# Experts in 1024-column pieces, and the first expert's up projections as plain float32 matmuls in column tiles

## The chip, the core and the metric

The kernel runs on one core of a Trainium2 chip. A core has five engines, each with a queue of its own: TensorE (PE; its weight loads are shown as PEld), VectorE (DVE), ScalarE (ACT), GpSimd (POOL) and SyncE (SP), which here issues nearly all DMAs. The metric is the device time of one execution in microseconds (us), median of several runs; lower is better.

## The reference

Two decoder layers over 256 tokens of width 1024. Each has a mixer (gated recurrence, short convolution, merge) and a feed-forward part: a dense SwiGLU in layer 0, eight SwiGLU experts of inner width 2816 in layer 1, two for each token. The change touches only the experts:

```python
logits = jnp.einsum('td,de->te', t, router_w)
top_vals, top_idx = lax.top_k(logits, TOP_K)          # TOP_K = 2 of 8
gates = sum(one_hot(top_idx, 8) * softmax(top_vals))
for e in range(N_EXPERTS):
    a = t @ w1[e]                                     # 1024 -> 2816
    b = t @ w3[e]                                     # 1024 -> 2816
    out = out + gates[:, e:e + 1] * ((jax.nn.silu(a) * b) @ w2[e])
```

All of it is float32, 34.6 MB of weights for each expert.

## The kernel before

**Numbers.** TensorE has a one-pass type, float32r, that keeps fewer bits than float32. The kernel keeps float32 accuracy by splitting each operand into a high part `hi` and a low part `lo`, both float32r, and adding three products: hi·hi, hi·lo, lo·hi. Weights are split when they arrive. `wload` (L73) issues the DMA of one piece of 1 MB (128 partitions x 2048 elements, tile `wraw`) from SyncE, ScalarE copies it to `whi` (L86), VectorE makes `wlo = wraw - whi` (L88).

**Buffers.** `whi` has three buffers and `wlo` two. The `wraw` pieces go round a ring: four of a pool and a number of larger tiles that are idle just then; `more` puts such tiles in, `less` takes them out before the tile gets a use of its own.

**The experts** (`moe`, L739 to L978). The routing gives each expert up to 128 slots. `gather` multiplies one-hot matrices `P` (tile `sg`, made by `hot` at L794) with the token rows and so collects the rows of two experts at once, transposed and already in parts: `xh` and `xl`, 1024 rows in 8 tiles `kt` x 256 slots (tiles `bu`/`fc` and `kk`/`qq`; copies at L826, L828, L830). Then for every expert and every piece of the inner width (`FCH`: five of 512 columns and one of 256) the program issues

- `up_proj` of w1 (the gate) into `ab[:, 0]`: slots stationary, 512 weight columns moving, three matmuls for each `kt` (L881, L882, L883), two loads of four `kt` each;
- `turn` of the piece before: four transposes on PE (L890) and the split of the result into `ahe`, `ale` on ACT and DVE (L50, L51);
- `up_proj` of w3 (the up projection) into `ab[:, 1]`;
- `down` of the piece before: three matmuls for each 128 rows of w2 and each half of the width (L906 to L908) into `ye`, which gathers over all pieces of an expert;
- the activation: Silu on ACT (L976), the product on DVE (L977).

`ab` has two buffers in PSUM, so the next piece's `ab` is another buffer. After an expert's last piece `gated` scales `ye` (L933, L934), and after each second expert one-hot products put the rows back (L925).

**Order.** The program issues in this order; a scheduler moves instructions of one engine against each other where data allow it. Each engine then runs its list strictly in order. Before the first expert, `late` computes gates and the largest slot count, which SyncE reads (L987) between two weight loads.

The scores of the mixer are plain float32 matmuls, both operands `F32`. `scores` has the only ones that write a part of the partitions:

```python
rows = slice(2 * m * b, 2 * m * b + m)
for i in range(4):
    nc.tensor.matmul(ps[rows, i, b, :], kk[g][:, i, ...], qv[:, i, b, m:2 * m], ...)
```

At L359 with m = 32 these are 32 columns of the array, at rows 0 to 31 (b = 0) and 64 to 95 (b = 1); with m = 64 there are 64 columns at rows 0 to 63. At L338 the loop `for i in range(4)` over two token tiles makes 8 matmuls of 128 columns in a row.

Of the kernel before, what the change touches and what calls it, by code (L numbers as in the profile page):

```python
# [27 lines left out]
FCH = [(c, min(512, FF - c)) for c in range(0, FF, 512)]  # L28


@with_exitstack
def trunk_kernel(ctx: ExitStack, tc: tile.TileContext, x, w_in, lower_bounds, hgrn_norm_w, conv_w,
# [39 lines left out]
    def wload(src2d, k0, nk, c0, ncol):  # L72
        """rows k0*128.. (nk tiles) x columns c0..c0+ncol, split -> hi, lo [128, nk, ncol]"""  # L73
# [100 lines left out]
    # mean squares of the rows of the residual stream, by halves of the width  # L174
# [45 lines left out]
    # ---- the residual stream times a norm's weight, as columns in parts, by halves of the width. The  # L220
    # norm's factor of a token is applied to what is made of them: rstd by token, rbc as a row for all. ----
# [35 lines left out]
    def bounds():  # L257
        """lower bounds of the forget gates: cumulated softmax over the layers, less the first"""
# [33 lines left out]
    # within a block of 4, s <= t  # L292
# [6 lines left out]
    # s in the first, t in the second half of a block of 2m; t of the second halves only  # L299
# [85 lines left out]
    # o = S^T v, normalised per head, gated; token-major  # L385
# [89 lines left out]
    def route_slots(t):  # L475
        """1 + slot of the token within each expert, 0 where not chosen"""
# [6 lines left out]
    # ================= mixer =================  # L483
    def mixer(l):
# [13 lines left out]
        # forget gate, key, query: [key, head, t] in two groups of four heads  # L498
# [21 lines left out]
        # scores, transposed: [s, head, t]  # L520
# [12 lines left out]
        # output gate, token-major: silu(g) * norm weight  # L533
# [10 lines left out]
        # merge gates  # L544
# [12 lines left out]
        # short convolution: [channel, t]  # L557
# [30 lines left out]
        # projections and merge: [d, t]  # L588
# [21 lines left out]
        for g in range(2):  # L610
# [20 lines left out]
            # a token tile after the other, the routing of the first beside the second  # L631
# [25 lines left out]
    # ================= dense SwiGLU =================  # L657
    def dense(l):
# [10 lines left out]
        def down(c0, n, ah, al, w, dh, cs):  # L669
            """columns cs of the weights w, to the half dh of the width"""  # L670
# [11 lines left out]
        for ci, (c0, n) in enumerate(FCH):  # L682
# [15 lines left out]
            else:  # L698
                # the last two: one half of the width after the other
# [22 lines left out]
    # ================= final norm =================  # L722
# [12 lines left out]
    # ================= top-2 expert SwiGLU =================  # L735
    def moe(l):
# [8 lines left out]
        # the factors of a row: of its normalisation, and its gates; by token and by slot  # L745
# [11 lines left out]
        def make_gates():  # L757
            """softmax over the two kept logits"""
# [17 lines left out]
        def late():  # L776
            """what only the scatter needs: the gates, and the largest number of tokens of an expert"""
# [8 lines left out]
        def slots(base):  # L786
            """all experts on their slots base .. base+127"""
# [23 lines left out]
            def gather(e2, first=False):  # L811
# [3 lines left out]
                # one-hot products of the parts: exact  # L815
# [16 lines left out]
                if first:  # L832
                    # the first token tile ahead of the routing of the second
# [40 lines left out]
            def up_proj(src, c0, n, o, xh, xl, es):  # L874
                nh = (KT * n + 2047) // 2048
                per = KT // nh
                for half in range(nh):
                    wh, wl = wload(src, half * per, per, c0, n)
                    for k in range(per):
                        kt = half * per + k  # L880
                        nc.tensor.matmul(o, xh[:, kt, es], wh[:, k, :], start=kt == 0, stop=False)  # L881
                        nc.tensor.matmul(o, xh[:, kt, es], wl[:, k, :], start=False, stop=False)  # L882
                        nc.tensor.matmul(o, xl[:, kt, es], wh[:, k, :], start=False, stop=kt == KT - 1)  # L883

            def turn(e, c0, n, ci, sa, ys):
                """gated activations [slot, f] -> their parts [f, slot]"""
# [4 lines left out]
                ah = big.tile([128, nt, 128], F32R, tag=f"st{ci % 2}1", name="ahe")  # L891
                al = big.tile([128, nt, 128], F32R, tag=f"st{ci % 2}2", name="ale")
# [3 lines left out]
            def down(e, c0, n, ah, al, ys, PT, halves=(0, 1)):  # L896
                nt = n // 128
                for d0, dn in ([(h * 512, 512) for h in halves] if n == 512 else [(0, 1024)]):
                    wh, wl = wload(expert_w2[j, e], c0 // 128, nt, d0, dn)
                    for dh in range(dn // 512):  # L900
                        for k in range(nt):
                            o = ys[d0 // 512 + dh]
                            ds_ = slice(dh * 512, dh * 512 + 512)
                            first = c0 == 0 and k == 0
                            end = c0 + n == FF and k == nt - 1
                            nc.tensor.matmul(o, ah[:, k, :], wh[:, k, ds_], start=first, stop=False)  # L906
                            nc.tensor.matmul(o, ah[:, k, :], wl[:, k, ds_], start=False, stop=False)  # L907
                            nc.tensor.matmul(o, al[:, k, :], wh[:, k, ds_], start=False, stop=end)  # L908
# [27 lines left out]
            pend = None  # L936
# [7 lines left out]
            d_gather, p_gather = last["gather"], last["prod"]  # L944
            for e in range(NE):
# [4 lines left out]
                for ci, (c0, n) in enumerate(FCH):  # L950
# [3 lines left out]
                    ab = psum.tile([128, 2, 512], F32, tag="mm", name="ab")  # L954
                    up_proj(expert_w1[j, e], c0, n, ab[:, 0, 0:n], xh, xl, es)
# [6 lines left out]
                    if base == 0 and e == 0 and ci == 4:  # L962
                        less("tokA")
                    if e == 0 and ci == 3:
                        less("v")
                        PT = hot_t()
                    if pend is not None:
                        pend = turn(*pend)
                    up_proj(expert_w3[j, e], c0, n, ab[:, 1, 0:n], xh, xl, es)
                    if e % 2 == 1 and e + 1 < NE and ci == 2:  # L970
                        less("fc", "qq")
                        nxt = gather(e // 2 + 1)
                    if pend is not None and not final:
# [54 lines left out]
```

## Time and profile before

| | us |
|---|---|
| median of 3 runs (lowest, highest) | 1619.73 (1618.6, 1619.83) |
| span of the profiled execution, first to last instruction | 1618.9 |
| PE busy | 1594.9 |
| PEld busy | 1427.5 |
| DVE busy | 1243.7 |
| ACT busy | 938.4 |
| POOL busy | 33.9 |

For the profiled execution only its span is given, no time of its own; it lies within the three runs' range and 0.8 us under their median. The experts are worked on from about 826 us to 1605 us. Matmuls are pipelined: the profile models their ends, so that a row of 0.39 us may be followed by the next start 0.23 us later. What a matmul costs in a dense stream is read from starts.

### The profile page before, as it was taken

The numbers are of one execution on the slowest core, as the hardware profiler recorded it, in microseconds if no ns is written. First come the engines' busy times: TensorE is split into PE (matmuls) and PEld (weight loads), VectorE is DVE, ScalarE is ACT, GpSimd is POOL, SyncE is SP. The second block draws the span as 40 slices with busy tenths as digits, with TensorE's granted clock in tenths as the row PEclk, the third lists the DMA queues.
The fourth block names the chain that finished last, engine by engine and source line by source line (L and its number), as shares of the span: only waits on it lengthen the run. The fifth ranks groups of instructions, "written<-read, shape, count | busy, mean of one in ns | idle before, by whom it ended". The sixth has DMA issues, their size and how long they took to land.

```text
span 1618.9 us, 23572 instructions
## 1 busy us (share of the span) xinstructions
PE 1594.9 (99%) x9858; PEld 1427.5 (88%) x9858; DVE 1243.7 (77%) x1182; ACT 938.4 (58%) x836; POOL 33.9 (2%) x51
## 2 busy tenths in 40 slices
PE   7999999999999999999999999999999999999997
PEld 7989999999999989999988888888888888888886
DVE  6964785655446965677678898888888888888886
ACT  6434343544335444334467777677776777767775
POOL 2000020000000000010000000000000000000000
PEclk9999999999999999999999999999999999999998
DMA  7544445555654554458568999999999999999992
GB/s 276 183 158 164 149 132 187 180 182 181 201 189 162 177 182 156 157 195 286 171 221 311 352 324 331 337 366 373 339 356 331 364 374 346 365 334 365 373 376 97
DMA packets 215939, 417.06 MB, mean 258 GB/s; under 512 B 6528, under 2 KB 25056, under 8 KB 215824
## 3 DMA queue, kind: packets, MB, share of 16 engines
q1 hardware_dynamic: 215408, 414.25, 73.1%
q8 instruction: 79, 1.29, 0.3%
q0 software_dynamic: 384, 1.21, 0.2%
q14 instruction: 36, 0.29, 0.0%
q10 hardware_dynamic: 32, 0.01, 0.0%
HBM read 414.40 MB, written 1.05 MB: 257 GB/s over the span
## 4 chain that ended last, share of the span: by engine, by line
PE 96%; DVE 2%; ACT 1%; DMA 1%; issue 0%; POOL 0%; SPq 0%; POOLq 0%; DVEq 0%
PE psb L128 11%; PE psb L130 11%; PE psb L132 11%; PE ab L882 10%; PE ab L883 10%; PE ab L881 9%; PE ye L908 5%; PE ye L906 5%; PE ye L907 5%; PE psa L149 2%; PE psa L151 2%; PE psa L150 2%; PE psl L365 1%; PE y L677 1%; PE y L678 1%; PE y L679 1%
## 5 line engine op out<-in xcount | busy, mean ns | idle before, releaser
L86 ACT ACTIVATE whi<-wraw 128x2048 fp32r<-128x2048 f32 (+1 forms) x456 | 760.5, 1679 | 507.8 <-PE psb L130 257.6
L88 DVE TENSOR_TENSOR wlo<-wraw,whi 128x2048 fp32r<-128x2048 f32 (+1 forms) x456 | 900.1, 1993 | 199.7 <-ACT whi L86 93.1
L128 PE MATMUL psb<-hlA,whi 128*128 128x256 f32 x1376 | 393.2, 286 | 2.7 <-ACT hlA L217 2.7
L130 PE MATMUL psb<-hlB,whi 128*128 128x256 f32 x1376 | 390.5, 284 | 0.5 <-DVE hlB L218 0.5
L132 PE MATMUL psb<-hlA,wlo 128*128 128x256 f32 x1376 | 390.3, 284 | 0.0
L128 PEld LDWEIGHTS psb<-hlA,whi 128*128 128x128 f32 x1376 | 264.4, 192 | 3.9 <-ACT hlA L217 3.1
L130 PEld LDWEIGHTS psb<-hlB,whi 128*128 128x128 f32 x1376 | 264.6, 192 | 1.1 <-DVE hlB L218 0.7
L132 PEld LDWEIGHTS psb<-hlA,wlo 128*128 128x128 f32 x1376 | 264.5, 192 | 0.2
L882 PE MATMUL ab<-wlo,bu 128*128 128x512 f32 (+1 forms) x384 | 144.2, 375 | 1.2 <-DVE wlo L88 1.2
L882 PE MATMUL ab<-wlo,fc 128*128 128x512 f32 (+1 forms) x384 | 144.5, 376 | 0.8 <-DVE wlo L88 0.8
L881 PE MATMUL ab<-whi,bu 128*128 128x512 f32 (+1 forms) x384 | 144.2, 376 | 0.0
L881 PE MATMUL ab<-whi,fc 128*128 128x512 f32 (+1 forms) x384 | 143.8, 374 | 0.0
L883 PE MATMUL ab<-whi,kk 128*128 128x512 f32 (+1 forms) x384 | 143.0, 372 | 0.0
L883 PE MATMUL ab<-whi,qq 128*128 128x512 f32 (+1 forms) x384 | 142.9, 372 | 0.0
L907 PE MATMUL ye<-wlo,ahe 128*128 128x512 f32 x352 | 137.7, 391 | 0.7 <-DVE wlo L88 0.7
L908 PE MATMUL ye<-whi,ale 128*128 128x512 f32 x352 | 136.9, 390 | 0.2
L906 PE MATMUL ye<-whi,ahe 128*128 128x512 f32 x352 | 136.6, 390 | 0.0
L882 PEld LDWEIGHTS ab<-wlo,bu 128*128 128x128 f32 x384 | 72.4, 189 | 14.4 <-DVE wlo L88 2.8
L882 PEld LDWEIGHTS ab<-wlo,fc 128*128 128x128 f32 x384 | 72.3, 188 | 14.4 <-DVE wlo L88 2.7
L881 PEld LDWEIGHTS ab<-whi,fc 128*128 128x128 f32 x384 | 72.3, 188 | 12.6
L881 PEld LDWEIGHTS ab<-whi,bu 128*128 128x128 f32 x384 | 72.3, 188 | 12.3
L883 PEld LDWEIGHTS ab<-whi,kk 128*128 128x128 f32 x384 | 72.4, 188 | 12.1
(243 smaller groups left out, 1867.1 us busy)
## 6 DMA issues: line engine op xcount, KB each, us to landing
wraw<-in_expert_w_dram SPq DMA_DIRECT2D x264, 1024.0 KB, 6.8
wraw<-in_w_in_dram SPq DMA_DIRECT2D x72, 1024.0 KB, 5.0
wraw<-in_dense_w_dram SPq DMA_DIRECT2D x33, 1024.0 KB, 5.0
wraw<-in_w_proj_conv_dram SPq DMA_DIRECT2D x8, 1024.0 KB, 5.0
wraw<-in_w_proj_hgrn_dram SPq DMA_DIRECT2D x8, 1024.0 KB, 5.0
wraw<-in_w_out_dram SPq DMA_DIRECT2D x8, 1024.0 KB, 5.0
xt<-in_x_dram SPq DMA_DIRECT2D x2, 512.0 KB, 4.7
out_dram<-bu SPq DMA_DIRECT2D x4, 256.0 KB, 2.9
```

The costliest lines, as they stand in the source:

```text
L86: nc.scalar.activation(hf[:, ks], rf[:, ks], AF.Copy)
L88: nc.vector.tensor_tensor(lf[:, ks], rf[:, ks], hf[:, ks].bitcast(F32), op=ALU.subtract)
L128: nc.tensor.matmul(o, wh[:, k, cs], hh[:, kt, :], start=first, stop=False, skip_group_check=True)
L130: nc.tensor.matmul(o, wh[:, k, cs], hl[:, kt, :], start=False, stop=False, skip_group_check=True)
L132: nc.tensor.matmul(o, wl[:, k, cs], hh[:, kt, :], start=False, stop=last, skip_group_check=True)
L149: nc.tensor.matmul(o, hh[:, kt, ts], wh[:, k, :], start=kt == 0, stop=False)
L881: nc.tensor.matmul(o, xh[:, kt, es], wh[:, k, :], start=kt == 0, stop=False)
L882: nc.tensor.matmul(o, xh[:, kt, es], wl[:, k, :], start=False, stop=False)
L883: nc.tensor.matmul(o, xl[:, kt, es], wh[:, k, :], start=False, stop=kt == KT - 1)
L906: nc.tensor.matmul(o, ah[:, k, :], wh[:, k, ds_], start=first, stop=False)
L907: nc.tensor.matmul(o, ah[:, k, :], wl[:, k, ds_], start=False, stop=False)
L908: nc.tensor.matmul(o, al[:, k, :], wh[:, k, ds_], start=False, stop=end)
```

## The change

The experts' pieces become 1024 columns wide (`WIDE`: 1024, 1024, 768). A load is two `kt` of up to 1024 columns, with rows of 4 KB instead of 2 KB in memory; the number of float32r matmuls of an expert stays the same. The gate and the up product of a piece are now two PSUM tiles `pa` and `pb` of the tag that had two buffers for `ab`, so one piece's pair fills both. A piece is activated, turned and fed to `down` in two halves (`p`), one directly behind the other.

The first expert's two up projections are done without splits: `xf = xh + xl` (one DVE addition, 128x1024, into tile `fc`), the raw weights `wraw` as the moving operand, both plain float32, one matmul instead of three for each `kt` and 512 columns. But each is cut by slots: for the gate into two matmuls of 64 slots, for the up projection into four of 32, each on its own columns of the array and its own partitions of the output. Experts 1 to 7 keep the splits. Comment lines that the change also takes out, and shifted line numbers, are left out here.

```diff
+WIDE = [(c, min(1024, FF - c)) for c in range(0, FF, 1024)]
...
+    def wraw(src2d, k0, nk, c0, ncol):
+        r = from_ring("raw", raws, [128, nk, ncol], F32)
+        nc.sync.dma_start(r, src2d[k0 * 128:(k0 + nk) * 128, c0:c0 + ncol].rearrange("(k p) c -> p k c", p=128))
+        return r
...
             def up_proj(src, c0, n, o, xh, xl, es):
-                nh = (KT * n + 2047) // 2048
-                per = KT // nh
-                for half in range(nh):
-                    wh, wl = wload(src, half * per, per, c0, n)
...
+                for part in range(KT // 2):
+                    wh, wl = wload(src, part * 2, 2, c0, n)
+                    for k in range(2):
+                        kt = part * 2 + k
+                        for p in range(0, n, 512):
+                            ps_ = slice(p, min(p + 512, n))
+                            op = o[:, p // 512, 0:ps_.stop - p]
+                            nc.tensor.matmul(op, xh[:, kt, es], wh[:, k, ps_], start=kt == 0, stop=False)
+                            nc.tensor.matmul(op, xh[:, kt, es], wl[:, k, ps_], start=False, stop=False)
+                            nc.tensor.matmul(op, xl[:, kt, es], wh[:, k, ps_], start=False, stop=kt == KT - 1)
+
+            def up_full(src, c0, n, o, xf, lane):
+                for part in range(KT // 2):
+                    w = wraw(src, part * 2, 2, c0, n)
+                    for k in range(2):
+                        kt = part * 2 + k
+                        for p in range(0, n, 512):
+                            ps_ = slice(p, min(p + 512, n))
+                            for c in range(0, 128, lane):
+                                nc.tensor.matmul(o[c:c + lane, p // 512, 0:ps_.stop - p], xf[:, kt, c:c + lane],
+                                                 w[:, k, ps_], start=kt == 0, stop=kt == KT - 1)
...
+            def down(e, c0, n, ah, al, ys, PT):
+                for k0 in range(0, n // 128, 2):
+                    wh, wl = wload(expert_w2[j, e], c0 // 128 + k0, 2, 0, 1024)
...
+            if base == 0:
+                less("fc")
+                xf = big8("fc", [128, KT, 128])
+                nc.vector.tensor_tensor(xf, nxt[0][:, :, 0:128].bitcast(F32), nxt[1][:, :, 0:128].bitcast(F32), op=ALU.add)
...
-                for ci, (c0, n) in enumerate(FCH):
+                for ci, (c0, n) in enumerate(WIDE):
...
+                    pa = psum.tile([128, 2, 512], F32, tag="mm", name="ab")
+                    if e == 0 and base == 0:
+                        up_full(expert_w1[j, e], c0, n, pa, xf, 64)
+                    else:
+                        up_proj(expert_w1[j, e], c0, n, pa, xh, xl, es)
...
+                    pend = [turn(*x) for x in pend]
+                    pb = psum.tile([128, 2, 512], F32, tag="mm", name="ab")
+                    if e == 0 and base == 0:
+                        up_full(expert_w3[j, e], c0, n, pb, xf, 32)
+                    else:
+                        up_proj(expert_w3[j, e], c0, n, pb, xh, xl, es)
...
+                    def acts():
+                        return [activate(e, c0, n, p, pa, pb) + (ys,) for p in range((n + 511) // 512)]
```

How the order of instructions moves is seen at three places. The first is PE where the first expert begins; `pr` are the slot factors, `pp` the slot counts, `ppt` transposes of the one-hot matrices, `bu`, `kk` the tiles of `xh`, `xl`. Before:

```order
L819 MATMUL pg<-sg_7747,hlB 128x256 x6
L869 MATMUL pr<-rg,sg_7747 128x1 x4
L881 MATMUL ab<-whi,bu 128x512
L882 MATMUL ab<-wlo,bu 128x512
L883 MATMUL ab<-whi,kk 128x512
```

and of the change, from the same place:

```order
L826 MATMUL pg<-sg_7747,hlB 128x256 x6
L876 MATMUL pr<-rg,sg_7747 128x1 x4
L789 MATMUL pp<-sel,ones 128x8 x2
L811 MATMUL ppt<-ident,sg_7747 128x128 x4
L902 MATMUL ab<-wraw,fc 64x512 x32
L902 MATMUL ab<-wraw,fc 32x512 x64
L902 MATMUL ab<-wraw,fc 64x512 x32
```

The slot counts and the first four transposes now stand ahead of the first expert's products. A piece of 1024 columns is 32 matmuls for the gate (8 `kt`, two halves, two tiles) and 64 for the up projection; the last piece (768) is 16 of 512 and 16 of 256 columns for the gate, 32 and 32 for the up projection.

The second place is DVE at the same time. Before, the splits of the first loads (`wlo`) stand between the gather's copies and behind them:

```order
L88 TENSOR_TENSOR wlo<-wraw,whi 128x512 x2
L830 CAST kk<-pg 128x512 x2
L88 TENSOR_TENSOR wlo<-wraw,whi 128x512
L830 CAST kk<-pg 128x512
L872 COPY sc<-pr 128x2
L88 TENSOR_TENSOR wlo<-wraw,whi 128x512
L794 TENSOR_SCALAR sg_7747<-iota,posm 128x128 x12
```

Of the change:

```order
L837 CAST kk<-pg 128x512 x3
L879 COPY sc<-pr 128x2
L975 TENSOR_TENSOR fc<-bu,kk 128x1024
L801 TENSOR_SCALAR sg_7747<-iota,posm 128x128 x12
```

The splits are gone there, and the addition that makes `xf` (tile `fc`) stands behind the last copy and the slot factors, ahead of the other experts' one-hot matrices.

The third place is DVE within expert 2, where `sae` are activations and `ale` the low parts of turned ones. Before:

```order
L977 SCALAR_TENSOR_TENSOR sae<-ab,sc,sae 128x512
L88 TENSOR_TENSOR wlo<-wraw,whi 128x2048 x5
L51 TENSOR_TENSOR ale<-pta,ahe 128x512
L88 TENSOR_TENSOR wlo<-wraw,whi 128x2048
L977 SCALAR_TENSOR_TENSOR sae<-ab,sc,sae 128x512
```

Of the change:

```order
L910 SCALAR_TENSOR_TENSOR sae<-ab,sc,sae 128x512 x2
L89 TENSOR_TENSOR wlo<-wraw,whi 128x2048 x4
L52 TENSOR_TENSOR ale<-pta,ahe 128x512 x2
L89 TENSOR_TENSOR wlo<-wraw,whi 128x2048 x3
```

Work between the splits now comes in pairs, half as often.

## Rows read from the trace of the kernel before

**Rows 1.** The profile's page: busy time by engine, clock digits, chain that ended last.

```profile
PE 1594.9 (99%) x9858; PEld 1427.5 (88%) x9858; DVE 1243.7 (77%) x1182; ACT 938.4 (58%) x836; POOL 33.9 (2%) x51
...
PEclk9999999999999999999999999999999999999998
...
PE 96%; DVE 2%; ACT 1%; DMA 1%; issue 0%; POOL 0%; SPq 0%; POOLq 0%; DVEq 0%
```

**Rows 2.** Windows: length, busy us (instructions) by engine, PE clock, DMA share, GB/s.

```profile
1050.00:1100.00 50.00, 50.00 (x228) 41.42 (x227) 44.41 (x25) 37.75 (x24) 0.00 (x0) 1.00 1.04 369
1100.00:1150.00 50.00, 49.61 (x248) 41.60 (x247) 45.08 (x27) 37.18 (x27) 0.00 (x0) 1.00 0.99 356
```

**Rows 3.** Timeline of PE, 999.7 to 1003 us: start us, us, instruction.

```profile
999.73 0.39 PE L882 MATMUL ab<-wlo,bu 128*128 128x512 f32 x1
999.96 0.39 PE L883 MATMUL ab<-whi,kk 128*128 128x512 f32 x1
...
1002.91 0.39 PE L906 MATMUL ye<-whi,ahe 128*128 128x512 f32 x1
```

**Rows 4.** Timeline of PE at 1135 and 1330 us; in brackets its idle time before.

```profile
1135.22 0.50 PE L882 MATMUL ab<-wlo,fc 128*128 128x512 f32 x1 [0.39 <-DVE wlo L88]
...
1330.43 0.50 PE L882 MATMUL ab<-wlo,bu 128*128 128x512 f32 x1 [0.39 <-DVE wlo L88]
```

**Rows 5.** Waits, 826 to 1619 us: in total us, times, longest us.

```profile
PEld ab L882 <- DVE wlo L88: 5.5, 14, 1.2
...
PE ab L882 <- DVE wlo L88: 2.0, 4, 0.8
PEld ye L907 <- DVE wlo L88: 2.0, 4, 0.8
```

**Rows 6.** Timeline of PE at 21.7 us: split products of 256 columns, plain float32.

```profile
21.67 0.28 PE L128 MATMUL psb<-hlA,whi 128*128 128x256 f32 x1
21.79 0.28 PE L130 MATMUL psb<-hlB,whi 128*128 128x256 f32 x1
...
22.04 0.59 PE L242 MATMUL prb<-dg,ones 128*128 128x256 f32 x2
22.47 0.23 PE L195 MATMUL pcp<-ident,prow 80*128 80x80 f32 x1
```

**Rows 7.** Timeline of PE: 128 and 64 moving columns, then the next start.

```profile
88.70 1.95 PE L338 MATMUL psd<-qq,kk 128*128 128x128 f32 x16
90.40 0.48 PE L149 MATMUL psa<-whi,hlA 128*128 128x512 f32 x1
...
95.94 1.89 PE L365 MATMUL psl<-qq,kk 128*128 128x64 f32 x16
97.64 0.48 PE L149 MATMUL psa<-whi,hlA 128*128 128x512 f32 x1
```

**Rows 8.** Timeline of PE: the matmuls in 32 and in 64 columns.

```profile
118.08 0.69 PE L359 MATMUL psl<-qq,kk 128*32 128x32 f32 x16
...
125.76 1.15 PE L359 MATMUL psl<-qq,kk 128*64 128x64 f32 x16
126.83 0.39 PE L128 MATMUL psb<-hlA,whi 128*128 128x256 f32 x1
```

**Rows 9.** Timeline of DVE and PE where the first expert begins, and at 839 us.

```profile
826.01 0.69 DVE L830 CAST kk<-pg 128x512 fp32r<-128x512 f32 x1
826.80 0.16 DVE L872 COPY sc<-pr 128x2 f32<-128x2 f32 x1
...
826.62 0.48 PE L881 MATMUL ab<-whi,bu 128*128 128x512 f32 x1
...
838.05 0.39 PE L881 MATMUL ab<-whi,bu 128*128 128x512 f32 x1
839.23 0.50 PE L882 MATMUL ab<-wlo,bu 128*128 128x512 f32 x1 [0.80 <-DVE wlo L88]
```

**Rows 10.** Groups on DVE by shape: count, busy us, mean ns, idle before.

```profile
L977 DVE SCALAR_TENSOR_TENSOR sae<-ab,sc,sae 128x512 f32<-128x512 f32 x40 | 29.7, 743 | 0.0
...
L316 DVE TENSOR_TENSOR kk<-kk,fc 128x1024 f32<-128x1024 f32 x4 | 4.9, 1215 | 0.0
```

**Rows 11.** Timeline of ACT and DVE in an undisturbed stretch, 1089 to 1097 us.

```profile
1089.20 1.92 ACT L86 ACTIVATE whi<-wraw 128x2048 fp32r<-128x2048 f32 x1 [0.80 <-PE ye L908]
1091.16 2.29 DVE L88 TENSOR_TENSOR wlo<-wraw,whi 128x2048 fp32r<-128x2048 f32 x1 [0.38 <-ACT whi L86]
1093.87 2.29 DVE L88 TENSOR_TENSOR wlo<-wraw,whi 128x2048 fp32r<-128x2048 f32 x1 [0.43 <-ACT whi L86]
```

**Rows 12.** Windows around the routing; columns as in the second group.

```profile
815.00:818.70 3.70, 2.98 (x22) 2.49 (x22) 2.05 (x8) 2.01 (x5) 0.00 (x0) 1.00 0.74 218
818.70:825.50 6.80, 6.02 (x30) 5.93 (x29) 4.88 (x16) 3.44 (x8) 0.70 (x1) 0.50 0.52 194
```

More of the change, by code (lines that the diff above doesn't have):

```diff
@@ L874, in up_proj @@
             def up_proj(src, c0, n, o, xh, xl, es):
-                nh = (KT * n + 2047) // 2048
-                per = KT // nh
-                for half in range(nh):
-                    wh, wl = wload(src, half * per, per, c0, n)
[L879 to L883, printed above, removed]
@@ L887, in turn, with activate @@
+            def activate(e, c0, n, p, pa, pb):
+                m = min(512, n - p * 512)
+                sa = big.tile([128, m], F32, tag=f"st{p}0", name="sae")
+                nc.scalar.activation(sa, pa[:, p, 0:m], AF.Silu, scale=sc[:, e, 0:1])
+                nc.vector.scalar_tensor_tensor(sa, pb[:, p, 0:m], sc[:, e, 0:1], sa, op0=ALU.mult, op1=ALU.mult)
+                return e, c0 + p * 512, m, p, sa
+            def turn(e, c0, n, p, sa, ys):
                 nt = n // 128
@@ L890, in turn @@
                     nc.tensor.transpose(ps[:, k, :], sa[:, k * 128:k * 128 + 128], ident)
-                ah = big.tile([128, nt, 128], F32R, tag=f"st{ci % 2}1", name="ahe")
-                al = big.tile([128, nt, 128], F32R, tag=f"st{ci % 2}2", name="ale")
+                ah = big.tile([128, nt, 128], F32R, tag=f"st{p}1", name="ahe")
+                al = big.tile([128, nt, 128], F32R, tag=f"st{p}2", name="ale")
                 split(ps, ah, al)
                 return e, c0, n, ah, al, ys
[L896 to L902, printed above, removed]
-                            ds_ = slice(dh * 512, dh * 512 + 512)
[L904 to L908, printed above, removed]
+            def down(e, c0, n, ah, al, ys, PT):
+                for k0 in range(0, n // 128, 2):
+                    wh, wl = wload(expert_w2[j, e], c0 // 128 + k0, 2, 0, 1024)
+                    for k in range(2):
+                        for dh in range(2):
+                            o = ys[dh]
+                            ds_ = slice(dh * 512, dh * 512 + 512)
+                            first = c0 == 0 and k0 + k == 0
+                            end = c0 + n == FF and k0 + k == n // 128 - 1
+                            nc.tensor.matmul(o, ah[:, k0 + k, :], wh[:, k, ds_], start=first, stop=False)
+                            nc.tensor.matmul(o, ah[:, k0 + k, :], wl[:, k, ds_], start=False, stop=False)
+                            nc.tensor.matmul(o, al[:, k0 + k, :], wh[:, k, ds_], start=False, stop=end)
                 if c0 + n == FF:
@@ L934, in gated @@
                 nc.vector.scalar_tensor_tensor(y[1], src, g, y[0].bitcast(F32), op0=ALU.mult, op1=ALU.subtract)
-            pend = None
+            pend = []
             PT = None
@@ L953, in slots @@
                         ring["fine"] = 5
-                    ab = psum.tile([128, 2, 512], F32, tag="mm", name="ab")
-                    up_proj(expert_w1[j, e], c0, n, ab[:, 0, 0:n], xh, xl, es)
+                    pa = psum.tile([128, 2, 512], F32, tag="mm", name="ab")
[3 more added lines that the diff above has]
+                        up_proj(expert_w1[j, e], c0, n, pa, xh, xl, es)
                     if e == 0 and ci == 0:
@@ L961, in slots @@
                                 late()
-                    if base == 0 and e == 0 and ci == 4:
+                    if base == 0 and e == 0 and ci == 2:
                         less("tokA")
-                    if e == 0 and ci == 3:
+                    if e == 0 and ci == 1:
                         less("v")
                         PT = hot_t()
-                    if pend is not None:
-                        pend = turn(*pend)
-                    up_proj(expert_w3[j, e], c0, n, ab[:, 1, 0:n], xh, xl, es)
@@ L970, in slots @@
-                    if e % 2 == 1 and e + 1 < NE and ci == 2:
-                        less("fc", "qq")
-                        nxt = gather(e // 2 + 1)
-                    if pend is not None and not final:
-                        down(*pend, PT)
-                    sa = big.tile([128, n], F32, tag=f"st{ci % 2}0", name="sae")
-                    nc.scalar.activation(sa, ab[:, 0, 0:n], AF.Silu, scale=sc[:, e, 0:1])
-                    nc.vector.scalar_tensor_tensor(sa, ab[:, 1, 0:n], sc[:, e, 0:1], sa, op0=ALU.mult, op1=ALU.mult)
@@ L978, in slots @@
-                    if final:
-                        down(*pend, PT, [0])
-                        end = turn(e, c0, n, ci, sa, ys)
-                        down(*pend, PT, [1])
-                        down(*end, PT)
-                    pend = (e, c0, n, ci, sa, ys)
+                    pend = [turn(*x) for x in pend]
[4 more added lines that the diff above has]
+                        up_proj(expert_w3[j, e], c0, n, pb, xh, xl, es)
@@ new lines, in slots @@
+                    if e % 2 == 1 and e + 1 < NE and ci == 1:
+                        less("fc", "qq") if base == 0 and e > 1 else less("qq")
+                        nxt = gather(e // 2 + 1)
+                    def acts():
+                        return [activate(e, c0, n, p, pa, pb) + (ys,) for p in range((n + 511) // 512)]
+                    if not final:
+                        for x in pend:
+                            down(*x, PT)
+                        pend = acts()
+                        continue
@@ L985, in moe @@
+                    here = acts()
+                    for i, x in enumerate(pend):
+                        down(*x, PT)
+                        here[i] = turn(*here[i])
+                    for x in here:
+                        down(*x, PT)
         slots(0)
```

1 line of the change is left out of this document (removed).

## The prediction

> **What bounds the kernel now.** First the page: PE is busy 99% of the span, at a full clock but for short stretches, and 96% of the chain that ended last is PE's [rows 1]. Busy time proves little for PE, whose ends are modelled, so I read the stage that the change touches. In windows of 50 us PE is busy 49.6 to 50.0, DVE about 45, ACT about 38; the DMA share is about 1.0 [rows 2], so DMA, too, could be the bound. What decides is the spacing of PE's starts: from 999.73 to 1002.91 us lie 14 intervals, so a split product of 512 columns costs 3.18 / 14 = 0.227 us, one like the other [rows 3]. A PE that waited for data would be irregular. A larger test: the same place in the work comes again after 1330.43 − 1135.22 = 195.2 us, two experts [rows 4]. Two experts hold 2 x (5 x 8 x 2 x 3) = 480 products of 512 columns in the up projections and 264 in `down`, 744 x 0.227 = 168.9 us, and 96 of 256 columns at 0.12 (21.79 − 21.67 [rows 6]), 11.5 us. Transposes, gather and scatter come on top. That is 180.4 of 195.2 us before these are counted. What PE waits for `wlo` over all eight experts is small: 5.5 + 2.0 + 2.0 us in the larger groups, partly the same time seen by weight load and matmul [rows 5]. So the experts run at PE's own pace, and whatever lightens DVE, ACT or DMA can give back some 10 us at most.
>
> **What the change removes.** In the first expert's two up projections: 240 products of 512 columns and 48 of 256, 240 x 0.227 + 48 x 0.12 = 60.3 us of PE. Also their splits on ACT and DVE, which the rows above show to be off the path.
>
> **What it adds on PE.** A plain float32 matmul is two records in the trace: the program has 8 at L338, the trace 16 [rows 7]. Two records of 256 columns take 22.47 − 22.04 = 0.43 us [rows 6]; 16 of 128 columns take 1.70 [rows 7], 0.106 each, the same price per column. So a record of 512 columns is 0.43 us, one of 256 0.215. The gate's tiles of 64 slots make 80 matmuls of 512 and 16 of 256 columns: 160 x 0.43 + 32 x 0.215 = 75.7 us of streaming. The up projection's tiles of 32 make twice as many: 151.4. A narrow tile does not stream faster: with 64 array columns, 16 records of 64 moving columns take 1.07 us [rows 8], 0.067 each, no less than 64 / 256 x 0.215 = 0.054.
>
> So all depends on whether streams in different column tiles overlap. The kernel before never shows it: its only change of tile, in the middle of the 16 records at 118.08 [rows 8], lies among streams so short that a weight load is as long. (A load of 128 columns takes 0.106: 64 moving columns at L365 go no faster than 128 at L338 [rows 7]. By share, an estimate, 32 columns take 0.027 and their stream, also by share, 32 / 256 x 0.215 = 0.027.) The ends:
>
> - every tile's stream beside the others: the gate 75.7 / 2, the up projection 151.4 / 4, 75.7 us together, 15.4 more than the 60.3 removed;
> - all one after the other: 227.1 us, 166.8 more.
>
> I take a value between. In every row PE starts matmuls in the program's order, and a tile's two records stand next to each other. The second cannot stream before the first has left the tile; only then can the next tile's first record start, beside it. So two streams run at any time, however many tiles there are: 227.1 / 2 = 113.5 us, **53.2 more**. Of the rows, those on weight loads are nearest: PEld is busy 88% of the span beside a PE busy 99% [rows 1], so the array takes in new weights while it streams. If the load at each change of tile shows, 96 x 0.053 + 192 x 0.027 = 10 us come on top; I leave them to the range.
>
> The Trainium skill (TensorE: Matmul & The Clock Gate, Part 3: Packing small matmuls) has a rule that speaks against the change: weight loads overlap running matmuls only when the row group differs. Column tiles share all rows. By it all 192 records of the gate and 384 of the up projection would show their loads, 192 x 0.053 + 384 x 0.027 = 20.5 us, and the sum would be 74 instead of 53. The rows on loads show overlap within one full-width tile, which the rule does not have, so I stay with 53.
>
> **The start.** The first product before starts at 826.62, with its first `kt` in place. Now it needs all of `xf`: the last gather copy ends at 826.70, the slot factors take 0.16 [rows 9], the addition as a 128x1024 row 1.22 [rows 10], so about 828.1: **1.5 more**, though `pp` and four transposes fill part of it. Against it, the wait at 839.23 (0.95 longer than the spacing of 0.227 [rows 9]) goes with the splits: **−1.0**.
>
> **Experts 1 to 7.** As many products, the same streams: nothing on PE. Longer DMA rows have PE's pace as their cover; if that cover went, DMA at its present rate would still deliver. The pairs on DVE: in a quiet stretch DVE idles 0.43 us of each 2.72 (1093.87 − 1091.16) and waits for ACT, which waits for a free `whi` [rows 11]. With three such buffers a split done 0.2 + 1.92 + 2.29 = 4.4 us after a buffer came free is needed only 5.4 us after it, 1.0 to spare. Two activations of 0.743 in a row [rows 10] are 1.49: more than 0.43 + 1.0 by 0.06. I count 0.1 us for each of three pieces of seven experts: **2**. Bounds: −8, if nearly all waits for `wlo` went; +10, if each pair also held up ACT's next split by its 0.5. One pair of `pa` and `pb` fills both PSUM buffers, but Silu reads `pa` while PE works on the up projection and `down`, some 20 us: nothing.
>
> **Sum.** 53.2 + 1.5 − 1.0 + 2 = 55.7 on the profiled span of 1618.9, 1674.6; the median stands 0.8 over that span: **1675 us**.
>
> **Rivals.**
>
> *Column tiles don't overlap.* The change then does not do what its tiles are for. For it: the 16 records of [rows 8] keep one pace over their change of tile, 16 in 0.69 with the last one's tail. Against: that pace is what loads alone would give. 166.8 in place of 53.2: 1789 us.
>
> *All tiles stream together.* 15.4 in place of 53.2: 1638 us. For it: no row forbids it. Against: a tile's two records stand side by side in PE's list. The skill's page on TensorE (Part 3 again) stands for this one: tiles start about 4 ns apart, measured for three column tiles of 32 as a gain of 2.38. No run here shows it.
>
> *The clock falls.* From 818.70 to 825.50 the granted clock was 0.50, that is 1.2 GHz, after 3.7 us in which PE ran few columns [rows 12]. If the up projection's narrow tiles had the same effect, its 75.7 us would double: 1751 us. Against: there PE was idle for 0.7 us and its matmuls had 8 columns; here it streams without pause.
>
> *It gets faster.* If narrow float32 tiles streamed one column per clock at full width (half the price seen, 0.215 us for a record) and all tiles ran together, 37.8 us would replace 60.3: 1600 us. It decides from 60.3 / 176 = 0.34 us for a record on, all tiles overlapping. Against: the 64-column tiles, whose records cost 0.067 where 0.027 would do.
>
> **How the numbers follow.** Chances: 0.45 for two at a time, 0.28 for no overlap, 0.18 for all together, 0.05 for the clock, 0.04 for the last. The likeliest gives 1675, its own range 1665 to 1690 (steady part −8 to +10, loads up to +10). No overlap and all together must both be in, since leaving out either leaves out too much with the last two: 1630 to 1795. 0.2% is about what a measurement of this kernel can tell from no change. Only the last rival can be faster: 0.03, and 0.01 for it to end about even; slower 0.96.
>
> **What would show it.** Right: the first expert's records of 512 columns in pairs, four in 0.86 us for the gate, eight in 1.72 for the up projection; about 113 us for both; first start near 828; the steady spacing still 0.227; two experts still about 195 us. Wrong: eight records in 0.86 us, or four in 1.72 for the gate; a clock of 0.5 there; a time per expert that grows by more than 2 us, which would mean that the pairs or the two PSUM tiles hold PE up.

## The result and the profile after

| | before | changed |
|---|---|---|
| median of 4 runs each on one chip (us) | 1619.78 (1618.6 to 1620.46) | 1663.85 (1662.02 to 1665.44) |
| ratio | | 1.0272, 95% interval 1.0257 to 1.0286 |
| span of the profiled execution (us) | 1618.9 | 1661.0 |

The change costs 44 us. The forecast was 1675 (55.7 more), so the size is near; but two of its terms are far off, in opposite directions.

The page of the changed kernel, with the lines that answer to [rows 1]:

```profile
PE 1623.2 (98%) x10146; PEld 1406.0 (85%) x10146; DVE 1197.3 (72%) x1170; ACT 897.6 (54%) x823; POOL 33.9 (2%) x51
...
PEclk9999999999999999999999999999998999989998
...
PE 96%; DVE 1%; ACT 1%; issue 1%; DMA 1%; POOL 0%; SPq 0%; POOLq 0%; DVEq 0%
```

PE is still the chain. What is new are digits of 8 in the clock line, in the second half, where the experts run: the granted clock falls there. So a place to look at, which the forecast did not name, stands in the page.

First the float32 part. Windows of the instructions of L902 alone (length, busy us and count of PE and of PEld, clock, DMA share, GB/s): the up projection of the first 1024 columns (tiles of 32), then the gate of the second 1024 (tiles of 64).

```profile
839.71:853.59 13.88, 13.88 (x131) 4.07 (x129) 1.00 0.67 228
853.59:867.47 13.88, 13.88 (x68) 4.50 (x64) 1.00 0.92 320
```

Sixteen products (8 `kt`, two halves) take 13.88 us whether they are cut in four tiles or in two: 0.868 each, which is two records of 0.43 [rows 6]. The weight loads of the up projection show how (timeline of PEld, start us, us, in brackets idle before):

```profile
842.32 0.13 PEld L902 LDWEIGHTS ab<-wraw,fc 128*32 128x32 f32 x4 [0.30 <-issue]
842.74 0.13 PEld L902 LDWEIGHTS ab<-wraw,fc 128*32 128x32 f32 x4 [0.30 <-issue]
```

Four loads together, and 0.42 us later the next four. The matmuls start in the same fours, some 7 ns apart (single starts in the trace: 842.313, 842.320, 842.327, 842.333, then 842.742): all tiles' first records run together, then all second ones. It is the rival "all tiles stream together".

Then the experts after the first. Windows as in [rows 2], 50 us behind the end of experts 1 and 3 and one quiet stretch:

```profile
1050.00:1100.00 50.00, 45.82 (x197) 36.66 (x196) 40.08 (x27) 31.39 (x23) 0.00 (x0) 0.97 0.81 281
1100.00:1150.00 50.00, 50.00 (x250) 41.88 (x249) 42.51 (x26) 38.16 (x28) 0.00 (x0) 1.00 1.00 384
1250.00:1300.00 50.00, 45.86 (x187) 36.25 (x186) 38.25 (x26) 30.70 (x23) 0.00 (x0) 0.90 0.77 276
```

In the quiet stretch PE starts 250 matmuls, behind expert 1 only 197 and behind expert 3 187. Both windows of [rows 2] have 228 or more, but the rows of expert 1 were put back just ahead of them; the window of before that takes in that place (1034.8 to 1040.4 us) has as many:

```profile
1030.00:1080.00 50.00, 50.00 (x228) 41.20 (x227) 44.75 (x30) 36.45 (x25) 0.00 (x0) 1.00 0.97 347
```

The timeline behind expert 1 in the changed kernel, all engines (`y` is the gated result of the odd expert, `psc` the products that put the rows back, called the scatter below, `xt` the residual rows):

```profile
1059.62 0.39 PE L935 MATMUL ye<-whi,ale 128*128 128x512 f32 x1
...
1060.11 1.52 PE L952 MATMUL psc<-y,v 128*128 128x512 f32 x4
...
1061.75 0.68 ACT L960 ACTIVATE y<-ye,sc 128x512 fp32r<-128x512 f32 x1
1061.89 2.29 DVE L89 TENSOR_TENSOR wlo<-wraw,whi 128x2048 fp32r<-128x2048 f32 x1 [1.05 <-ACT whi L87]
...
1064.10 1.28 DVE L954 TENSOR_TENSOR xt<-xt,psc 128x512 f32<-128x512 f32 x2
...
1064.84 1.22 PE L952 MATMUL psc<-tokA,v 128*128 128x512 f32 x2 [3.21 <-DVE xt L954]
...
1067.14 1.16 PE L952 MATMUL psc<-y,v 128*128 128x512 f32 x3
...
1067.80 1.27 ACT L909 ACTIVATE sae<-ab,sc 128x512 f32<-128x512 f32 x2 [3.57 <-PE psc L952]
...
1069.12 0.50 PE L889 MATMUL ab<-whi,fc 128*128 128x512 f32 x1 [0.83 <-ACT sae L909]
```

Read it backwards. PE's next `ab` (the next piece's `pa`) at 1069.12 waits for the Silu that writes `sae`; Silu had waited 3.57 us for the scatter's matmuls; these had waited 3.21 us for `xt`, which frees their buffer in PSUM (the memory that matmuls write) and stood on DVE behind a split of 2.29. So twelve scatter products run with no other work among them. The same place of the kernel before, behind expert 5:

```profile
1425.83 0.62 PE L925 MATMUL psc<-y,v 128*128 128x512 f32 x2
...
1427.43 0.62 PE L925 MATMUL psc<-y,v 128*128 128x512 f32 x2
...
1430.57 0.62 PE L925 MATMUL psc<-tokA,v 128*128 128x512 f32 x2
```

Between them PE starts 16 products of the next `ab`, five and eleven (1426.29 to 1430.34): the second buffer of `ab` gave it something to do. And the stall has a sequel (windows behind expert 5; behind expert 1 it is shorter, as shown below):

```profile
1466.90:1470.60 3.70, 1.83 (x6) 0.60 (x4) 2.21 (x2) 3.70 (x4) 0.00 (x0) 1.00 0.99 386
1470.60:1480.80 10.20, 7.93 (x18) 5.77 (x19) 7.48 (x9) 2.26 (x3) 0.00 (x0) 0.50 0.59 210
1480.80:1485.00 4.20, 4.20 (x20) 3.48 (x19) 1.42 (x1) 2.56 (x2) 0.00 (x0) 1.00 0.00 0
```

After 3.7 us in which PE started 6 matmuls, the granted clock is 0.50 (1.2 GHz) for 10.2 us, in which it starts 18; then full again. Both together give the theory tested below: the float32 part costs about 15, the wide pieces about 27, nearly all of it behind experts 1, 3 and 5. The trace bears out the place: from its own first product to that of the next expert, expert 2 takes 103.7 us and experts 4 and 6 take 105.1 each, against 96.4, 96.8 and 96.8 before, 23.9 more together.

The reason for the second: the second half of `y` uses the tags `st00` and `st10`, which are also the tags of `sae`. So the next expert's Silu can't write before the scatter has read `y`. This was so before as well, but there Silu held one of two `ab` buffers; now `pa` and `pb` are both, and the next `pa` needs the buffer that this Silu reads.

### The profile page after: what moved, and what is told of

Same layout as the page of the kernel before. It is cut to its first block, busy times and chain, and to the rows that moved or that the text cites. A ratio compares the mean times of both kernels' runs of the same rounds, so it can differ in the third digit from the quotient of the medians.

```text
span 1661.0 us, 24158 instructions
## 1 busy us (share of the span) xinstructions
PE 1623.2 (98%) x10146; PEld 1406.0 (85%) x10146; DVE 1197.3 (72%) x1170; ACT 897.6 (54%) x823; POOL 33.9 (2%) x51
## 4 chain that ended last, share of the span: by engine, by line
PE 96%; DVE 1%; ACT 1%; issue 1%; DMA 1%; POOL 0%; SPq 0%; POOLq 0%; DVEq 0%
PE psb L135 11%; PE psb L137 11%; PE psb L139 11%; PE ab L890 9%; PE ab L889 8%; PE ab L891 8%; PE ye L934 5%; PE ye L933 5%; PE ye L935 5%; PE ab L902 5%; PE psa L156 2%; PE psa L158 2%; PE psa L157 2%; PE psl L372 1%; PE y L684 1%; PE y L685 1%
## 5 line engine op out<-in xcount | busy, mean ns | idle before, releaser
L87 ACT ACTIVATE whi<-wraw 128x2048 fp32r<-128x2048 f32 (+2 forms) x443 | 720.4, 1639 | 588.1 <-PE psb L137 257.7
L89 DVE TENSOR_TENSOR wlo<-wraw,whi 128x2048 fp32r<-128x2048 f32 (+2 forms) x443 | 851.6, 1941 | 238.1 <-ACT whi L87 131.0
L933 PE MATMUL ye<-whi,ahe 128*128 128x512 f32 x352 | 129.0, 391 | 0.0
L889 PE MATMUL ab<-whi,bu 128*128 128x512 f32 (+1 forms) x288 | 108.6, 377 | 0.8 <-ACT sae L909 0.8
L890 PE MATMUL ab<-wlo,bu 128*128 128x512 f32 (+1 forms) x288 | 108.4, 376 | 0.8 <-DVE wlo L89 0.8
L891 PE MATMUL ab<-whi,kk 128*128 128x512 f32 (+1 forms) x288 | 107.8, 374 | 0.0
L891 PEld LDWEIGHTS ab<-whi,qq 128*128 128x128 f32 x384 | 72.6, 189 | 12.5
L902 PE MATMUL ab<-wraw,fc 128*32 128x512 f32 (+3 forms) x576 | 78.0, 558 | 0.5 <-DVE fc L975 0.5
L934 PEld LDWEIGHTS ye<-wlo,ahe 128*128 128x128 f32 x352 | 66.1, 188 | 14.4 <-DVE wlo L89 0.9
```

Of the source, the lines that this page charges most:

```text
L87: nc.scalar.activation(hf[:, ks], rf[:, ks], AF.Copy)
L89: nc.vector.tensor_tensor(lf[:, ks], rf[:, ks], hf[:, ks].bitcast(F32), op=ALU.subtract)
L889: nc.tensor.matmul(op, xh[:, kt, es], wh[:, k, ps_], start=kt == 0, stop=False)
L890: nc.tensor.matmul(op, xh[:, kt, es], wl[:, k, ps_], start=False, stop=False)
L891: nc.tensor.matmul(op, xl[:, kt, es], wh[:, k, ps_], start=False, stop=kt == KT - 1)
L902: nc.tensor.matmul(o[c:c + lane, p // 512, 0:ps_.stop - p], xf[:, kt, c:c + lane], w[:, k, ps_], start=kt == 0, stop=kt == KT - 1)
```

## The experiments

Nine kernels ran, each beside the kernel before on the same chip. Chips differ a little (before: 1619.8 to 1623.0), so ratios to before are compared; 0.001 is 1.6 us.

**Each part alone.** One kernel keeps the wide pieces and gives the first expert its splits back:

```diff
-                    if e == 0 and base == 0:
-                        up_full(expert_w1[j, e], c0, n, pa, xf, 64)
-                    else:
-                        up_proj(expert_w1[j, e], c0, n, pa, xh, xl, es)
+                    up_proj(expert_w1[j, e], c0, n, pa, xh, xl, es)
```

(the same for `pb`, and no `xf`). 

> The changed kernel with the first expert's up projections in split float32r again, as before; the pieces stay 1024 columns wide. Theory T (float32 part +15.4 us, because all column tiles stream together; wide pieces about +27, because the scatters behind experts 1, 3 and 5 stand in one block and PE stalls and its clock falls there): 1664 - 15.4 = about 1648 us, and the three half-clock stretches near 1065, 1270 and 1475 us stay. Rival R (the prediction's step: two streams at a time, +53 for the float32 part, wide pieces +2): about 1610 to 1622 us.

Measured: 1649.91 us, 1.0178 (1.0161 to 1.0195), so 28.8 over before, and 15.2 under the changed kernel by the ratios.

The other is the kernel before, with `xf` and `up_full` for its pieces of 512 columns:

```diff
-                    up_proj(expert_w1[j, e], c0, n, ab[:, 0, 0:n], xh, xl, es)
+                    if e == 0 and base == 0:
+                        up_full(expert_w1[j, e], c0, n, ab[:, 0, 0:n], xf, 64)
+                    else:
+                        up_proj(expert_w1[j, e], c0, n, ab[:, 0, 0:n], xh, xl, es)
```

> The kernel before with its 512-column pieces; only the first expert's two up projections in plain float32, gate in tiles of 64 slots and up projection in tiles of 32. Theory T: +15.4 us of streaming, about 1635 us; about 3 us less if the stretch of half clock near 819 us, which the changed kernel does not show, goes away here too; no stalls behind experts 1, 3 and 5. Rival R: +44 to +53, 1664 to 1673 us.

Measured: 1640.03 us, 1.0118 (1.0102 to 1.0135), 19.1 over before. Its windows, eight products in four tiles, eight in two, and then 50 us around the end of expert 1:

```profile
835.78:842.78 7.00, 7.00 (x66) 1.97 (x64) 1.00 1.05 394
842.78:849.80 7.02, 7.02 (x36) 2.21 (x32) 1.00 1.02 354
...
1050.00:1100.00 50.00, 50.00 (x228) 41.23 (x227) 44.80 (x30) 35.87 (x25) 0.00 (x0) 1.00 0.97 345
```

The price for a product, 0.875, is near that of the changed kernel, and no stall follows expert 1. The 3.7 us above 15.4 are partly the clock. The window of the first float32 records:

```profile
827.50:830.90 3.40, 3.40 (x10) 0.97 (x8) 3.40 (x19) 2.39 (x4) 0.00 (x0) 0.50 0.00 0
```

The clock is at half for 3.4 us, which costs 1.7; in the changed kernel it was full there. Of the other 2.0, 88 products at 0.875 instead of 0.86 make 1.3, and the first product stands 0.4 later than before (827.06). The gain of 3 us from the clock did not come. That 15.2 and 28.8 add up to the 44.0 of the whole change says nothing, since 15.2 is the difference of the two. The two parts measured apart make 19.1 + 28.8 = 47.9, 3.9 too many; half clock over the first products costs the float32 part alone 1.7, and the wide pieces alone about as much (3.5 us at 0.51):

```profile
826.90:830.40 3.50, 3.50 (x9) 2.81 (x10) 3.16 (x6) 0.00 (x0) 0.00 (x0) 0.51 0.40 89
```

The rival (44 to 53 for the float32 part) is out.

**The buffer of y.** In the changed kernel the second half of `y` gets a buffer of its own, taken from the weight ring:

```diff
+        less("sg8")
...
-                        odd = [big.tile([128, 512], F32R, tag=tag, name="y")
-                               for tag in (("st01", "st02"), ("st00", "st10"))[dh]]
+                        if dh == 0:
+                            odd = [big.tile([128, 512], F32R, tag=tag, name="y") for tag in ("st01", "st02")]
+                        else:
+                            y2 = big.tile([128, 2, 512], F32R, tag="sg8", name="y")
+                            odd = [y2[:, q] for q in range(2)]
```

> The changed kernel, but the second half of an odd expert's gated result has a buffer of its own instead of the tags st00 and st10 that the activations sae of the next piece use; the weight ring has one large buffer less for it. Theory T (these tags tie the next expert's Silu, and by it the only pair of PSUM tiles, to the end of the scatter): the stalls of about 9 us behind experts 1, 3 and 5 go, with their half clock: 1664 - 27 = about 1637 us. Rival P (the single pair of PSUM tiles alone makes the stall, since the next piece's pa waits for the activation anyway): the stalls stay, 1660 to 1664 us.

Measured: 1645.81 us, 1.0155 (1.0138 to 1.0172): 19.0 less than the changed kernel, short of the 27 expected. The windows behind experts 1 and 5:

```profile
1050.00:1100.00 50.00, 49.26 (x222) 39.66 (x221) 44.22 (x30) 33.71 (x24) 0.00 (x0) 1.00 0.88 314
...
1452.00:1463.00 11.00, 10.26 (x44) 7.67 (x43) 8.94 (x6) 6.99 (x6) 0.00 (x0) 1.00 0.95 360
```

The clock is 1.00 and PE busy 49.26 of 50. Among what is left are short waits for `wlo`:

```profile
1057.99 0.50 PE L935 MATMUL ye<-wlo,ahe 128*128 128x512 f32 x1 [0.53 <-DVE wlo L89]
...
1067.50 0.50 PE L891 MATMUL ab<-wlo,fc 128*128 128x512 f32 x1 [0.21 <-DVE wlo L89]
```

The control gives the same buffer to the first half of `y` and leaves the second in `st00` and `st10`:

```diff
-                        if dh == 0:
-                            odd = [big.tile([128, 512], F32R, tag=tag, name="y") for tag in ("st01", "st02")]
+                        if dh == 1:
+                            odd = [big.tile([128, 512], F32R, tag=tag, name="y") for tag in ("st00", "st10")]
```

> A control for the own buffer: it is given to the first half of the odd expert's gated result (so its tags st01, st02 are left alone), and the second half keeps st00 and st10. The weight ring has the same one buffer less. Theory T (only st00 and st10, the tags of sae, matter): the stalls stay, 1660 to 1667 us, with half-clock stretches. Rival (any buffer of its own, or the shorter ring, made the gain): about 1646 us.

Measured: 1668.27 us, 1.0271 (1.0242 to 1.03): nothing gained. The stall is there:

```profile
1069.98 1.22 PE L956 MATMUL psc<-tokA,v 128*128 128x512 f32 x2 [3.20 <-DVE xt L958]
...
1074.54 0.80 PE L890 MATMUL ab<-whi,fc 128*128 128x512 f32 x1 [0.78 <-ACT sae L910]
```

So it is these two tags, not the ring nor any spare buffer. That the single pair of PSUM tiles is the other half of the cause is read from the trace of before; a second pair was not tried.

The own buffer with split weights for the first expert too (both edits above): 

> The changed kernel with split float32r for the first expert too, and with the second half of an odd expert's gated result in a buffer of its own: wide pieces alone, without the shared tags. Theory T (the two costs add up): 1649.9 - 18.1 (what the own buffer was worth with the float32 part in place) = about 1632 us, 11 above before; what is left of the wide pieces are the waits for wlo behind the experts. Rival R (the own buffer helps only because the float32 part is there): 1645 us or more.

Measured: 1627.71 us, 1.0031 (1.0018 to 1.0043), 5 over before and 23.8 under wide pieces without the buffer, more than the 18.1 expected. A part of the difference is the clock behind expert 1, which in the kernel with wide pieces alone fell for longer than in the changed kernel (windows of the one, then of the other):

```profile
1050.00:1060.20 10.20, 8.41 (x24) 6.17 (x25) 6.93 (x9) 2.29 (x4) 0.00 (x0) 0.67 0.66 225
```

```profile
1064.40:1067.80 3.40, 2.96 (x7) 2.39 (x8) 3.40 (x4) 0.00 (x0) 0.00 (x0) 0.50 0.74 248
```

A mean of 0.67 over 10.2 us is 6.7 us at half clock, against 3.4. Another part lies ahead of the stalls: the first product of expert 1 stands at 916.2 with wide pieces alone and at 913.9 with the own buffer, and the half clock over the first products, shown above, is only in the former. What the tags cost is cleaner between the first product of expert 1 and that of expert 7 (PE's starts, profiled executions):

| kernel | us |
|---|---|
| before | 585.7 |
| float32 part alone | 585.7 |
| changed | 611.5 |
| changed, own buffer for the second half of `y` | 592.5 |
| changed, own buffer for the first half (control) | 614.2 |
| wide pieces alone | 613.1 |
| wide pieces, own buffer for the second half | 592.7 |

So the own buffer takes back 19.0 of 25.8 and 20.4 of 27.4; about 7 stay.

Last, what stays (5 us by the medians). The work between the splits is written apart:

```diff
-                    pend = [turn(*x) for x in pend]
+                    pend[0:1] = [turn(*x) for x in pend[0:1]]
...
+                    pend[1:] = [turn(*x) for x in pend[1:]]
...
-                        for x in pend:
-                            down(*x, PT)
-                        pend = acts()
+                        new = []
+                        for p in range((n + 511) // 512):
+                            new.append(activate(e, c0, n, p, pa, pb) + (ys,))
+                            if pend:
+                                down(*pend[p], PT)
+                        pend = new
```

> Wide pieces with the split weights and the own buffer for y, and the work between the splits written apart: the second half is turned behind the up projection, each half is activated directly before one half of the down products. Theory (what is left, 4.7 us, is wlo late behind pairs on DVE): the three waits of 1.1 us and the three of 1.4 us behind the experts shrink, 1621 to 1626 us. Rival (the scheduler still puts the pairs together, or the waits come from the gather's and the scatter's own DVE work): 1627 to 1629 us.

Measured: 1628.31 us, 1.0040 (1.0026 to 1.0053), no better. The scheduler still put both activations of a piece side by side on DVE, two in one row:

```profile
1131.64 1.41 DVE L911 SCALAR_TENSOR_TENSOR sae<-ab,sc,sae 128x512 f32<-128x512 f32 x2 [1.18 <-PE ab L892]
```

So the pairs were not taken apart there, and what makes the last 5 us is not settled. No version here beats the kernel before.

**The column tiles.** First none at all: 128 slots in one matmul.

```diff
-                        up_full(expert_w1[j, e], c0, n, pa, xf, 64)
+                        up_full(expert_w1[j, e], c0, n, pa, xf, 128)
...
-                        up_full(expert_w3[j, e], c0, n, pb, xf, 32)
+                        up_full(expert_w3[j, e], c0, n, pb, xf, 128)
```

> The changed kernel with both float32 up projections of the first expert without column tiles: 128 slots in one matmul. Theory T (the first records of all tiles start together, then all second records, so the tiles change nothing): 1664 us within 1 to 2. Rival (tiles cost something for each change of tile or each extra load, or stream at another rate than full width): faster by 5 us or more.

Measured: 1664.28 us, 1.0267 (1.025 to 1.0284): the tiles neither gain nor cost more than these medians can tell, some 3 us. The traces hint at a small cost: the first expert takes 102.3 us to the next expert's first product without tiles, 0.9 of it from half clock at its start, and 104.1 with them; a later first product (828.5 against 825.8) hides it. Ten records at full width take 4.29 us (the counts take in a record at each edge):

```profile
831.16:835.45 4.29, 4.29 (x12) 1.90 (x10) 1.00 0.30 63
```

Then the order of the list. Four matmuls of one tile in a row:

```diff
-                    for k in range(2):
-                        kt = part * 2 + k
-                        for p in range(0, n, 512):
-                            ps_ = slice(p, min(p + 512, n))
-                            for c in range(0, 128, lane):
+                    for c in range(0, 128, lane):
+                        for k in range(2):
+                            kt = part * 2 + k
+                            for p in range(0, n, 512):
+                                ps_ = slice(p, min(p + 512, n))
```

> The changed kernel with the float32 matmuls of a load written tile by tile: the four of one column tile (two kt, two halves of 512 columns) in a row, then those of the next tile. Theory T1 (PE starts in the order of its list, so only neighbours of different tiles run together): of a tile's 8 records only one lies beside the next tile's first, 14 steps of 0.43 us a load for the gate instead of 8, and 28 for the up projection instead of 8: +28 and +95, about 1787 us. Theory T2 (each tile has a queue that lets it run ahead of the others by several matmuls): as in the changed kernel, 1664 us.

Measured: 1714.64 us, 1.0579 (1.0559 to 1.06), 50 over the changed kernel: neither theory. The windows of gate and up projection:

```profile
827.35:843.34 15.99, 15.99 (x64) 6.04 (x65) 1.00 0.54 177
843.34:873.09 29.75, 29.75 (x129) 8.75 (x128) 1.00 0.35 117
```

The up projection's 128 records, 16 runs of 8, take 29.75 us instead of 13.88 together or 55 one after the other. That is 1.86 us for a run with the last one's tail in it; from run to run it is 1.75 (starts at 845.087, 846.835, 848.582, 850.328), four steps of 0.43. So the next tile begins when the one before has four of its eight records left, and two streams run at any time, which is what the forecast had for the order as it stands in the change. Two matmuls of a tile in a row tell whether that is a fixed number:

```diff
-                        for p in range(0, n, 512):
-                            ps_ = slice(p, min(p + 512, n))
-                            for c in range(0, 128, lane):
+                        for c in range(0, 128, lane):
+                            for p in range(0, n, 512):
+                                ps_ = slice(p, min(p + 512, n))
```

> The changed kernel with the two matmuls of a column tile for one kt (its two halves of 512 columns) in a row, then those of the next tile. Written four in a row, a tile's successor began some 4.3 steps of 0.43 us after it, when about 4 of its 8 records were left. Theory T3 (a tile may have about two matmuls, four records, accepted ahead, and the list goes on behind them): two in a row cost next to nothing, 1664 to 1668 us. Rival (a tile's successor begins when half of its run is done): 2.2 steps for each tile, 8.7 instead of 4 steps for the up projection of one kt and 4.7 instead of 4 for the gate, +50 as with four in a row, about 1715 us.

Measured: 1668.09 us, 1.0292 (1.0276 to 1.0308), 3 over the changed kernel, though the two intervals overlap. The windows, up projection and gate:

```profile
840.23:854.18 13.95, 13.95 (x131) 5.32 (x129) 1.00 0.69 228
854.18:868.11 13.93, 13.93 (x67) 5.54 (x64) 1.00 0.93 325
```

13.95 instead of 13.88: it is a fixed number. The list goes on past about two float32 matmuls that a tile has still to stream.

## Why the prediction was near, and where it was wrong

**PE at its own pace, and what goes** (right): 60.3 us out, PE bound, DVE and ACT lighter for nothing. The price of a record, 0.43, held in every tile width.

**"Two streams at any time": 53.2** (wrong, the step that failed first). It took "the second cannot stream before the first has left the tile" to mean that the list stops there. The second record does wait, but the list goes on, to the next tile: up to about two matmuls of one tile may wait, as the two reorderings showed. All tiles stream together, 15.4 by the rows; 15.2 measured in the wide kernel, 19.1 in the narrow one with its half clock. The rival had 0.18. The Trainium skill (TensorE: Matmul & The Clock Gate, Part 3: Packing small matmuls) said so, with starts some 4 ns apart; the trace agrees, with 7. The Trainium skill's other rule there, that loads overlap only when the row group differs, does not hold here: in 13.88 us of streaming lie 4.07 us of loads for tiles that share all rows, and 32 records at 0.429 without tiles would take 13.73.

**The start: +1.5 − 1.0** (small, not confirmed). The addition lasted 1.22, as priced, but the first product stood at 825.83, not 828; in the other kernels it moved between 824 and 829 with what the routing ahead of it did and where the clock was at half. The half clock of [rows 12] was absent in the changed kernel's execution:

```profile
818.70:825.50 6.80, 5.42 (x41) 4.69 (x40) 4.63 (x12) 3.88 (x6) 0.43 (x1) 1.00 0.35 143
```

**Experts 1 to 7: 2, within −8 to +10** (wrong by far): 28.8 for the wide pieces. The sentence that failed is that Silu reads `pa` while PE has 20 us of other work, "nothing". It weighed when Silu's input is ready and not when its output buffer is free. `sae` is written over `y`, which the scatter reads at the end of every second expert. Some 20 of the 28.8 go with those two tags, stall and clock together (19.0 and 20.4 from expert 1 to expert 7; the 23.8 between the medians has some 2 of the start in it). The term that the step did work out, pairs of work on DVE, is at most what is left, 5 by the medians and 7 in that stretch, inside its bounds; it is not shown to be the pairs.

**The sum**: 15.2 + 28.8 in place of 53.2 + 0.5 + 2. The total came near because one error was 38 too high and the other 27 too low. That is luck and says nothing for the working; 1663.85 even lies just under the 1665 to 1690 that the likeliest case gave itself. Of the signs that the forecast named, two spoke against it at once: eight records in 0.86 us for the up projection, and a time per expert that grew by more than 2 us (from the first product of expert 3 to that of expert 5 it took 204.7, not 195).

## What to carry to other kernels

Cutting a float32 product into column tiles that all read the same moving data changes next to nothing by itself: the tiles run side by side, and the price stays that of two records at full width, above that of three float32r products (0.86 against 0.68 us for 512 columns). When a change takes away a second buffer, follow every wait of the instruction that frees the remaining one, its output's buffer too: a shared tag that cost nothing before becomes the path. And a stall of some microseconds on PE was paid for twice here, once as idle time and once by the clock that fell behind it.

## What the runs showed of the hardware that was not expected

Plain float32 matmuls in different column tiles start about 7 ns apart, records of one tile 0.43 us apart, and PE's list runs about two matmuls (four records) ahead of a tile: two in a row cost 0.07 us in 13.88, four in a row 15.9. The clock fell to 1.2 GHz for 10.2 us after 3.7 us with 1.83 us of PE work, and not after waits of 0.2 to 0.5 us in the kernel with the own buffer.
